# Full-row score products with zero rows, and SSM inputs from an ordered copy

## The chip, the cores and the metric

One NeuronCore of a Trainium2 chip runs the whole program in one launch. The metric is the device time of one execution in microseconds (us); less is better. Engines are named as in the profile: PE is TensorE (PEld its weight loads), DVE is VectorE, ACT is ScalarE, POOL is GpSimd and SP the queue that issues most transfers.

## What is computed

The reference is a stack of three transformer layers on 512 tokens of width 1024 (528 with 16 meta tokens in the first two layers). Each layer is a feed-forward block, a mixer and a second feed-forward block. Only the mixers matter here:

- Mixer A (first layer): differential attention, 8 heads with two score maps each, `logits = q·k * scale + bias` over 64 numbers a head, softmax, `p0 - lam*p1`, times V. All queries see the 16 meta keys besides the real ones.
- Mixer B (second layer): sparse latent attention with 16 heads, which shares the helper for the 16 meta keys.
- Mixer C (third layer): windowed attention with 12 heads in 3 patterns, scores over 64 numbers a head again, beside a state-space branch (SSM) whose input is `u = x @ w[:, :512]`, cross-attention and gates.

```python
bu_re = jnp.einsum('blgh,gph->blgp', uf, bbar_re)     # u in 32 groups of 16
logits = jnp.einsum("bqhmd,bkhmd->bmhqk", qb, k).astype(jnp.float32) * scale + bias
pd = p[:, 0] - lam_full * p[:, 1]
```

## The kernel before

Every fp32 operand is split into a high and a low part (ACT casts the high part, DVE subtracts for the low one), and a product is three matmuls: high·high, high·low, low·high. The helper `mm3` (L108, L110, L112) does this for projections; where "a projection" is counted below, it is 24 matmuls of 512 columns. `loadw` fetches a weight through `st` (L85), casts it (L88, ACT) and subtracts (L90, DVE); its pool `wp` holds four weight pairs.

Scores have only 64 rows to contract, so the kernel packs. `stack_q` puts the high part of a head's q in 64 rows and the low part in the other 64 of one tile; `stack_k` puts the high part of k in both halves, and the low part in a third tile, in the head's own 64 rows. `scores` then is two matmuls: L475 over all 128 rows (both parts of q with the high part of k) and L476 over 64 rows alone (the high part of q with the low part of k). The two add up in one PSUM bank:

```python
s.nc.tensor.matmul(p, Q[b][:, cq], K[b][:, ck], start=True, stop=False)       # L475
s.nc.tensor.matmul(p, Q[b][r, cq], K[2][r, ck], start=False, stop=True)       # L476, r = 64 rows
```

`pv` multiplies probabilities and values. Its first two matmuls are those of the 16 meta keys: L836 over 48 rows (high and low part of the probabilities, `PM`, at rows 0 and 32) and L837 over 16 rows. The rest (L841) has 128 rows. Mixer B has its own matmul over the 48-row tiles (L1098). `pm_tile` (L817) makes these tiles and clears them once.

In mixer C two heads go with each index j. A slot (j, b) is the attention of head b of j: for four blocks of 128 queries and three patterns a score pair into one of three banks, a DVE instruction that adds the bias strip and keeps the running maximum (L1511), one exponential per block on ACT (L1517), a reciprocal and a scaling on DVE (L1519, L1520); then transposes on PE (L1546), the split of what they give (L455 on ACT, L456 on DVE), and the products with V (L1552), at the end `fold`. A slot pair, slots (j, 0) and (j, 1), has 24 score pairs, 54 transposes and 68 products with V.

The program text of mixer C is: projections of j = 0, V of j = 0 (`vproj`, L1485), slots (0, 0) and (0, 1), `ssm_u` for the first half of the SSM inputs, projections and V of j = 1, slots (1, 0) and (1, 1), `ssm_u` for the second half, then the SSM itself (L1711, L1724 and on) with gate projections between its parts. `ssm_u` has positions in four classes modulo 4, since the SSM wants four neighbouring positions side by side. It takes every fourth column of `xh` and `xl` as the stationary operand, so that a weight load reads with a stride of four elements, and multiplies with 256 columns of the weight: 96 matmuls for each half (L1690).

A scheduler orders each engine's instructions from this text; an engine then works through its own list in order. So matmuls that wait for nothing (projections, `ssm_u`) are put between those of a slot that wait for DVE and ACT. It can do this only if their weight is loaded, which needs one of the four buffers of `wp`.

Of the kernel before, what the change touches and what calls it, by code (L numbers as in the profile page):

```python
# [8 lines left out]
F32 = mybir.dt.float32  # L9
# [25 lines left out]
class Kern:  # L35
# [430 lines left out]
    def stack_k(s, K, p, c):  # L466

        for b, (r, o) in enumerate(HALVES):
            s.split(K[b][r, c], K[2][r, c], p[r])
            s.nc.scalar.copy(K[b][o, c], p[r])  # L470

    def scores(s, p, Q, K, b, cq, ck):

        r = HALVES[b][0]
        s.nc.tensor.matmul(p, Q[b][:, cq], K[b][:, ck], start=True, stop=False)  # L475
        s.nc.tensor.matmul(p, Q[b][r, cq], K[2][r, ck], start=False, stop=True)  # L476

# [101 lines left out]
    def mixer_a(s, x, gnext):  # L579
# [6 lines left out]
        with ExitStack() as es:  # L586
# [29 lines left out]
            om = o1.tile([128, 128], F32, name="om")  # L616
            sm = o1.tile([16, 2, 8], F32, name="sm")
# [13 lines left out]
            def fin(hd, i, ac):  # L631
                if i < 2:
                    sd[hd, i] = [o2.tile([128, 528], F32R, tag="%s%d" % ("qk"[i], a), name="%ss" % "qk"[i])
                                 for a in range(2 + i)]
                if i == 0:
# [30 lines left out]
                else:  # L666
# [8 lines left out]
                    v.tensor_copy(VM[:, hd], raw[:, 0:16])  # L675
                    mh, ml = vms[hd % 3], o2.tile([16, 128], F32R, tag="vml", name="vml", bufs=3)
                    s.split(mh[0:16], ml, pt[:16, :128])
                    nc.scalar.copy(mh[32:48], pt[:16, :128])
# [46 lines left out]
            def meta():  # L725

                MB = o1.tile([16, 16, 16], F32, name="mb")
                for q in range(16):
# [3 lines left out]
                                                        ap=[[w - 1, 16], [1, 16]]))  # L732
                P = o1.tile([16, 16, 16], F32, name="pmeta")
                bc = (lambda q: q.unsqueeze(2).to_broadcast((16, q.shape[1], 16)))
# [31 lines left out]
                for hd in range(8):  # L766
                    nc.tensor.matmul(p[:, hd * 16:hd * 16 + 16], vt[hd // 4][:, hd % 4 * 128:hd % 4 * 128 + 128], PmT[:, hd * 16:hd * 16 + 16], start=True,
                                     stop=True)
                nc.scalar.copy(om, p[:, :128])
                sq = s.t528("sq", "sqm")[:, :128]  # L770
# [3 lines left out]
                r = s.rsqrt([(p, 0, 128)], 128, sq, lnexp=True)  # L774
                v.scalar_tensor_tensor(om, om, pr[:, 2:3], r, op0=ALU.mult, op1=ALU.mult)

            s.run(T, proj(0), 3)
            s.banks(**ATTN)
            s.run(T, proj(1)[2:], 0)
            for hd in range(8):  # L780
                attn(hd)
                if hd < 7:
                    s.run(T, proj(hd + 1)[:2 if hd < 6 else 3], 0)
                if hd < 5:
                    s.run(T, proj(hd + 2)[2:], 0)
                if hd == 6:
                    meta()
# [43 lines left out]
    def pv(s, po, PT, PM, vh, vl, mh, ml, vsl, msl, M, hv):  # L831
# [596 lines left out]
    def mixer_c(s, x, gnext):  # L1428
# [15 lines left out]
        with ExitStack() as es0:  # L1444
            c0 = es0.enter_context(tc.tile_pool(name="c0", bufs=1))
            DO = [c0.tile([128, 2, 512], F32R, name="do%d" % i) for i in range(2)]
            cu = es0.enter_context(tc.tile_pool(name="cu", bufs=2))
            todo = []
# [4 lines left out]
            with ExitStack() as es:  # L1453
# [3 lines left out]
                s.stat = es.enter_context(tc.tile_pool(name="dst", bufs=12))  # L1457
                qk, V = {}, {}

                def job(kind, gr, j):  # L1460
# [7 lines left out]
                    def fin(acs):  # L1468
                        t = [d1.tile([128, 512], F32R, tag="%s%d%d" % (kind, gr, q), name="%ss" % kind)
                             for q in range(2 if kind == "q" else 3)]  # L1470
# [202 lines left out]

    def ssm_u(s, pool, xh, xl, hf):

        nc = s.nc
        v = nc.vector
        ws = [s.loadw(s.I["w_u"][hf, a], 1024) for a in range(2)]
        U4 = pool.tile([128, 1024], F32, tag="u4", name="u4")
        U4 = U4.rearrange("p (g r h) -> p g r h", r=4, h=16)  # L1680
        for rp in range(2):
            pu = s.bank()
            for r in (2 * rp, 2 * rp + 1):
                for k in range(8):
                    wh, wl = ws[k // 4]
                    sl = slice((k % 4) * 256, (k % 4) * 256 + 256)
# [5 lines left out]
            for r in (2 * rp, 2 * rp + 1):  # L1692
                q = pu[:, r % 2 * 256:r % 2 * 256 + 256].rearrange("p (g h) -> p g h", g=16)
                if r % 2:
                    v.tensor_copy(U4[:, :, 3 - r], q)
                else:
                    nc.scalar.copy(U4[:, :, 3 - r], q)
        return U4
# [139 lines left out]
def prepare(v):  # L1838
    def t(a):
        return np.ascontiguousarray(a)  # L1840
# [48 lines left out]
    w = v["w_in_2"][0]  # L1889
    A["w_u"] = t(w[:, :512].reshape(2, 4, 128, 2, 256).transpose(3, 0, 2, 1, 4).reshape(2, 2, 128, 1024))  # L1890
    A["w_q"] = pack(w[:, 512:1280])
# [56 lines left out]
```

## Time and profile before

| | |
|---|---|
| runs | 3524.14, 3529.34, 3533.30 us; median 3529.34 |
| the profiled execution | 3530.96 us, its span 3529.2 us |
| PE busy, share of the span | 3385.9 us, 96% |
| DVE, ACT, POOL | 75%, 46%, 9% |
| mean granted clock of PE | 0.975 of full speed |

Times in rows are counted from the start of the span. A matmul's own duration overlaps with the next one's; the pace of PE is the distance from one start to the next. What stands as idle before an instruction is told with what released it.

### The profile page before, as it was taken

How to read it: one execution, taken by the hardware profiler on the slowest of the kernel's cores; microseconds unless marked ns; L12 is line 12 of the kernel's file. 1: busy time of each engine (PE TensorE's matmuls, PEld its weight loads, DVE VectorE, ACT ScalarE, POOL GpSimd, SP SyncE). 2: the span in 40 equal slices, each digit the busy share in tenths (PEclk: the TensorE clock that was granted, in tenths of full speed). 3: DMA queues.
4: the chain of work that ended last, by engine and by line, in shares of the span. 5: the costliest groups of instructions: out<-in, count | busy, mean ns of one | idle time of the engine just before them, and what ended most of it. 6: DMA issues, size and time to landing. Idle time of an engine off the chain costs nothing.

```text
span 3529.2 us, 60108 instructions
## 1 busy us (share of the span) xinstructions
PE 3385.9 (96%) x23568; PEld 3121.1 (88%) x23568; DVE 2647.1 (75%) x5495; ACT 1640.7 (46%) x3026; POOL 311.2 (9%) x494
## 2 busy tenths in 40 slices
PE   7999999999999999988999799999999999999998
PEld 7999888899999999977878699999998878889997
DVE  8777766699978987688978588787774555388776
ACT  5444566544445444555654344444453433344443
POOL 0100122100000000054520001000000000010000
PEclk9999999999999999988999899999998999999999
DMA  3532322123323432231212334233232233242331
GB/s 132 165 100 84 96 64 67 47 83 111 116 91 106 138 110 91 73 116 41 61 66 81 110 113 129 92 109 103 92 97 74 71 120 101 80 130 92 106 102 60
DMA packets 133645, 336.95 MB, mean 95 GB/s; under 512 B 27042, under 2 KB 39106, under 8 KB 133360
## 3 DMA queue, kind: packets, MB, share of 16 engines
q1 hardware_dynamic: 114336, 311.38, 28.3%
q0 software_dynamic: 19024, 21.72, 2.1%
q8 instruction: 185, 3.03, 0.4%
q14 instruction: 100, 0.82, 0.1%
HBM read 320.00 MB, written 24.35 MB: 98 GB/s over the span
## 4 chain that ended last, share of the span: by engine, by line
PE 86%; DVE 7%; DMA 3%; ACT 2%; issue 2%; POOL 0%; SPq 0%; DVEq 0%; ACTq 0%; POOLq 0%
PE bank L401 33%; PE bank L108 14%; PE bank L110 14%; PE bank L112 14%; PE bank L1690 1%; PE bank L476 1%; PE bank L1088 1%; PE bank L1485 1%; PE bank L475 1%; PE bank L1101 1%; DVE wl L90 1%; PE bank L841 1%; DMA xr<-in_oh 1%; PE bank L1008 1%; DMA xr<-dP 0%
## 5 line engine op out<-in xcount | busy, mean ns | idle before, releaser
L401 PE MATMUL bank<-xh,wl 128*128 128x264 f32 (+1 forms) x1920 | 539.8, 284 | 13.1 <-DVE wl L359 13.1
L88 ACT CAST wh<-st 128x1024 fp32r<-128x1024 f32 (+5 forms) x385 | 319.2, 840 | 497.2 <-PE bank L110 266.7
L401 PE MATMUL bank<-xh,wh 128*128 128x264 f32 (+1 forms) x1920 | 543.3, 284 | 4.5 <-ACT wh L358 4.5
L90 DVE TENSOR_TENSOR wl<-st,wh 128x1024 fp32r<-128x1024 f32 (+4 forms) x373 | 363.9, 982 | 151.1 <-ACT wh L88 150.2
L110 PE MATMUL bank<-gl,wh 128*128 128x264 f32 (+2 forms) x1638 | 447.1, 316 | 0.0
L112 PE MATMUL bank<-gh,wl 128*128 128x264 f32 (+2 forms) x1638 | 444.0, 316 | 0.0
L108 PE MATMUL bank<-gh,wh 128*128 128x264 f32 (+2 forms) x1638 | 442.4, 318 | 0.4 <-DVE h L261 0.3
L108 PE MATMUL bank<-xh,wh 128*128 128x264 f32 (+3 forms) x1344 | 416.6, 325 | 10.6 <-ACT xh L455 3.2
L110 PE MATMUL bank<-xl,wh 128*128 128x264 f32 (+3 forms) x1344 | 425.1, 322 | 0.1
L112 PE MATMUL bank<-xh,wl 128*128 128x264 f32 (+3 forms) x1344 | 420.0, 319 | 0.0
L401 PE MATMUL bank<-xl,wh 128*128 128x264 f32 (+1 forms) x1440 | 408.1, 284 | 0.0
L401 PEld LDWEIGHTS bank<-xh,wl 128*128 128x128 f32 x1920 | 362.1, 190 | 14.4 <-DVE wl L359 13.5
L401 PEld LDWEIGHTS bank<-xh,wh 128*128 128x128 f32 x1920 | 363.7, 190 | 6.2 <-ACT wh L358 5.6
L401 PE MATMUL bank<-xq,wah 128*128 128x264 f32 (+1 forms) x1920 | 361.6, 284 | 0.5 <-ACT cc L406 0.3
L401 PEld LDWEIGHTS bank<-xq,wah 128*128 128x128 f32 x1920 | 299.8, 190 | 2.9 <-ACT sl L410 0.6
L110 PEld LDWEIGHTS bank<-gl,wh 128*128 128x128 f32 x1638 | 280.7, 189 | 21.8 <-issue 1.3
L108 PEld LDWEIGHTS bank<-gh,wh 128*128 128x128 f32 x1638 | 278.8, 189 | 22.3 <-ACT wah L358 1.1
L112 PEld LDWEIGHTS bank<-gh,wl 128*128 128x128 f32 x1638 | 279.0, 188 | 21.5 <-issue 1.6
L108 PEld LDWEIGHTS bank<-xh,wh 128*128 128x128 f32 (+1 forms) x1344 | 250.7, 192 | 35.2 <-ACT xh L455 3.6
L401 PEld LDWEIGHTS bank<-xl,wh 128*128 128x128 f32 x1440 | 272.7, 189 | 0.8 <-issue 0.5
L110 PEld LDWEIGHTS bank<-xl,wh 128*128 128x128 f32 (+1 forms) x1344 | 255.7, 191 | 20.1 <-issue 2.1
L401 PE MATMUL bank<-xq,wal 128*128 128x264 f32 (+1 forms) x960 | 271.6, 283 | 0.0
(591 smaller groups left out, 7681.7 us busy)
## 6 DMA issues: line engine op xcount, KB each, us to landing
st<-in_wi SPq DMA_DIRECT2D x144, 512.0 KB, 4.1
fu<-in_wi SPq DMA_DIRECT2D x120, 512.0 KB, 3.5
st<-in_wo SPq DMA_DIRECT2D x96, 384.0 KB, 3.1
st<-in_wo SPq DMA_DIRECT2D x96, 320.0 KB, 3.0
st<-in_a_w_in SPq DMA_DIRECT2D x24, 512.0 KB, 3.5
st<-in_w_out SPq DMA_DIRECT2D x24, 512.0 KB, 3.5
st<-in_w_g SPq DMA_DIRECT2D x24, 512.0 KB, 3.5
strip<-kA SPq DMA_DIRECT2D x32, 264.0 KB, 2.8
```

The source lines that it names most:

```text
L88: nc.scalar.copy(wh[:rows, :n], st[:rows, :n])
L90: s.wl.tensor_tensor(wl[:rows, :n], st[:rows, :n], wh[:rows, :n].bitcast(F32), op=ALU.subtract)
L108: nc.tensor.matmul(p[:m], a, xh(k, t0, n), start=st, stop=False)
L110: nc.tensor.matmul(p[:m], a, xl(k, t0, n), start=False, stop=False)
L112: nc.tensor.matmul(p[:m], b, xh(k, t0, n), start=False, stop=en)
L401: nc.tensor.matmul(B, a[:, w], q[c][:, k], start=first and k == 0 and z == 0, stop=k == 3 and z == 2, skip_group_check=not first)
L475: s.nc.tensor.matmul(p, Q[b][:, cq], K[b][:, ck], start=True, stop=False)
L476: s.nc.tensor.matmul(p, Q[b][r, cq], K[2][r, ck], start=False, stop=True)
L841: nc.tensor.matmul(po[:M, c], a[:, vsl(j)], q[:, k], start=False, stop=j == 0 and n == 2)
L1008: nc.tensor.matmul(pv[:n, z * 256:z * 256 + 256], c[:, k, t0:t0 + n], wv[:, k * 256:k * 256 + 256], start=q == 0, stop=q == 5)
L1088: nc.tensor.matmul(ps[0][:, :n], q[:, k * 512 + i * 128:k * 512 + i * 128 + 128], c[:, k, k0:k0 + n], start=z == 0, stop=z == 5)
L1101: nc.tensor.matmul(po[:, hv], vs[:, j, m], PT[i // 2][q][:, j * 256:j * 256 + 256], start=False, stop=j == 0 and q == 1)
```

## The change

The low part of k is kept in two tiles, one for each head of a pair, 128 rows high: 64 rows hold it, the other 64 are set to zero once (`low_keys`, by POOL) and never written again. The second score matmul takes all 128 rows. The tiles of the meta keys and their probabilities become 128 rows high with zeros below, so both meta matmuls take 128 rows, in mixer B too. Some small tiles of `meta` in mixer A now borrow room from tiles that exist. In mixer C `ssm_u` is called once, for both halves, after the last slot and after the pools of the attention are closed: for each of the eight k it copies `xh` (ACT) and `xl` (DVE) into tiles in which the four classes are contiguous, and multiplies with 512 columns.

```diff
@@ stack_k, scores
-            s.split(K[b][r, c], K[2][r, c], p[r])
+            s.split(K[b][r, c], K[2 + b][r, c], p[r])
...
-        s.nc.tensor.matmul(p, Q[b][r, cq], K[2][r, ck], start=False, stop=True)
+        s.nc.tensor.matmul(p, Q[b][:, cq], K[2 + b][:, ck], start=False, stop=True)
+    def low_keys(s, pool, n, name):
+        ts = [pool.tile([128, n], F32R, name="%s%d" % (name, b)) for b in range(2)]
+        for t, (_, o) in zip(ts, HALVES):
+            s.nc.gpsimd.memset(t[o].bitcast(F32), 0.0)
+        return ts
@@ mixer_a
-            vms = [s.pm_tile(o1, 128, "vm%d" % i) for i in range(3)]
+            vms = [[s.pm_tile(o1, 128, "vm%d%d" % (i, a)) for a in range(2)] for i in range(3)]
+            KL = [s.low_keys(o1, 528, "kl%d" % i) for i in range(2)]
@@ pm_tile, pv
-        t = pool.tile([48, n], F32R, name=name)
+        t = pool.tile([128, n], F32R, name=name)
...
-        nc.tensor.matmul(po[:M, c], ml[:, msl], PM[0:16, c], start=False, stop=False)
+        nc.tensor.matmul(po[:M, c], ml[:, msl], PM[:, c], start=False, stop=False)
@@ mixer_c
+                KL = [s.low_keys(d1, 512, "kl%d" % gr) for gr in range(3)]
...
-                U4 = [s.ssm_u(cu, xh, xl, 0)]
...
                 slot(1, 1)
-                U4.append(s.ssm_u(cu, xh, xl, 1))
+                s.banks(m=[0, 1, 2, 3])
+            cu = es0.enter_context(tc.tile_pool(name="cu", bufs=2))
+            with tc.tile_pool(name="xp", bufs=2) as xp:
+                U4 = s.ssm_u(cu, xp, xh, xl)
@@ ssm_u
-                    ah = xh[:, k].rearrange("p (m r) -> p r m", r=4)[:, r]
-                    al = xl[:, k].rearrange("p (m r) -> p r m", r=4)[:, r]
-                    for z, (a, b) in enumerate(((ah, wh), (ah, wl), (al, wh))):
-                        nc.tensor.matmul(pu[:, r % 2 * 256:r % 2 * 256 + 256], a, b[:, sl], start=k == 0 and z == 0,
-                                         stop=k == 7 and z == 2)
+        pu = [s.bank() for _ in range(4)]
+        for kc in range(4):
+            wh, wl = s.loadw(s.I["w_u"][kc], 1024)
+            for a in range(2):
+                k = 2 * kc + a
+                X = [xp.tile([128, 4, 128], F32R, tag="xp%d" % i, name="xp%d" % i) for i in range(2)]
+                nc.scalar.copy(X[0], xh[:, k].rearrange("p (m r) -> p r m", r=4).bitcast(F32))
+                v.tensor_copy(X[1], xl[:, k].rearrange("p (m r) -> p r m", r=4).bitcast(F32))
+                c = slice(a * 512, a * 512 + 512)
+                for r in range(4):
+                    for z, (x, w) in enumerate(((0, wh), (0, wl), (1, wh))):
+                        nc.tensor.matmul(pu[r], X[x][:, r], w[:, c], start=k == 0 and z == 0, stop=k == 7 and z == 2)
```

In the three mixers' score and meta matmuls the scheduler leaves the order as it was, but for a few rows near mixer A's end. In mixer C it does not. The first place is PE's list from the first scores of slot (1, 0) on; `wh`, `wl`, `xh` and `xl` belong to `ssm_u`, `ks` and `kl` are keys, `qs` queries. Before:

```order
L475 MATMUL bank4_77<-ks_30206,qs_30170 128x256
L476 MATMUL bank4_77<-ks_30208,qs_30170 128x256
L475 MATMUL bank2_75<-ks_30056,qs_30020 128x256
L476 MATMUL bank2_75<-ks_30058,qs_30020 128x256
L475 MATMUL bank3_76<-ks_30131,qs_30095 128x256
L476 MATMUL bank3_76<-ks_30133,qs_30095 128x256
L1690 MATMUL bank0_73<-wh_30694,xh_28669 128x256
L1690 MATMUL bank0_73<-wl_30696,xh_28669 128x256
L1690 MATMUL bank0_73<-wh_30694,xl_28670 128x256
```

The same place in the changed kernel, where L474 and L475 are the two score matmuls:

```order
L474 MATMUL bank4_77<-ks_30094,qs_30058 128x256
L475 MATMUL bank4_77<-kl20_29061,qs_30058 128x256
L474 MATMUL bank2_75<-ks_29946,qs_29910 128x256
L475 MATMUL bank2_75<-kl00_29053,qs_29910 128x256
L474 MATMUL bank3_76<-ks_30020,qs_29984 128x256
L475 MATMUL bank3_76<-kl10_29057,qs_29984 128x256
L474 MATMUL bank2_75<-ks_29946,qs_29910 128x256
L475 MATMUL bank2_75<-kl00_29053,qs_29910 128x256
L474 MATMUL bank3_76<-ks_30020,qs_29984 128x256
L475 MATMUL bank3_76<-kl10_29057,qs_29984 128x256
```

Where 96 matmuls of `ssm_u` and 48 of two gate projections stood between the scores and products of slots (1, 0) and (1, 1), there is now nothing of either kind: PE's list has the slots alone, then 96 matmuls of `ssm_u`, then a projection (21 rows), 8 transposes of the SSM, a projection and 8 transposes. In slots (0, 0) and (0, 1) the 144 matmuls of the j = 1 projections stay: 48 among the first seven score pairs, then none for some three fifths of the slot pair's instructions, then 96.

The second place is ACT's list at the end of slot (1, 1) in the changed kernel; `dth` is the high part of transposed probabilities, `xp0` the ordered copy of `xh`, `do0` the attention's output, `wh` a gate's weight:

```order
L455 CAST dth_30551<-bank5_78 128x512
L455 CAST dth_30551<-bank6_79 128x384
L861 COPY fold_30574<-bank7_80 64x512
L1696 CAST xp0_30597<-xh_28666 128x512
L1696 CAST xp0_30613<-xh_28666 128x512
L455 CAST do0_29039<-fold_30574 64x512
L1696 CAST xp0_30635<-xh_28666 128x512
L1696 CAST xp0_30651<-xh_28666 128x512
L88 CAST wh_30945<-st_30943 128x1024
```

The first copy stands behind the `fold` of the last slot, which reads the bank that the last products with V fill. The weights of `ssm_u` were cast earlier, three among the projections of j = 1 and one after V; all four pairs stay in `wp` until `ssm_u` has used them, and the gates' weights come behind.

## Rows read from the trace of the kernel before

**Rows 1.** The page: the chain of work that ended last, by engine.

```profile
PE 86%; DVE 7%; DMA 3%; ACT 2%; issue 2%; POOL 0%; SPq 0%; DVEq 0%; ACTq 0%; POOLq 0%
```

**Rows 2.** Timeline of PE in mixer A: start us, duration, line, out<-in, shape.

```profile
426.02 0.34 PE L475 MATMUL bank<-ks,qs 128*128 128x400 f32 x1
426.29 0.44 PE L476 MATMUL bank<-ks,qs 64*128 64x400 f32 x1
426.67 0.39 PE L108 MATMUL bank<-xh,wh 128*128 128x264 f32 x1
426.89 0.29 PE L110 MATMUL bank<-xl,wh 128*128 128x264 f32 x1
```

**Rows 3.** Timeline of PE in mixer C, where a 128-row matmul parts a pair.

```profile
2719.54 0.28 PE L475 MATMUL bank<-ks,qs 128*128 128x256 f32 x1
2719.65 0.28 PE L1552 MATMUL bank<-dth,vs 128*128 128x256 f32 x1
2719.87 0.38 PE L476 MATMUL bank<-ks,qs 64*128 64x256 f32 x1
```

**Rows 4.** Timeline of PE in mixer A at the meta matmuls.

```profile
517.26 0.38 PE L836 MATMUL bank<-pm,vm 48*128 48x256 f32 x1
517.57 0.38 PE L837 MATMUL bank<-pm,vml 16*128 16x256 f32 x1
517.88 0.50 PE L841 MATMUL bank<-pt,vh 128*128 128x256 f32 x2
```

**Rows 5.** Views of three lines: count, ns min/median/max, first and last start, forms.

```profile
L476 PE MATMUL bank<-ks,qs x128: 378/385/792, 419.8 to 2837.0; 64*128 64x256 f32 x48, 64*128 64x264 f32 x32, 64*128 64x400 f32 x16, 64*128 64x272 f32 x16
L837 PE MATMUL bank<-pm,vml x16: 377/380/576, 442.4 to 685.1; 16*128 16x256 f32 x16
L1098 PE MATMUL bank<-pm,vm x32: 378/381/384, 1612.7 to 1831.9; 48*128 48x256 f32 x32
```

**Rows 6.** Windows in mixers A, B: length, PE, PEld, DVE, ACT, POOL busy; clock.

```profile
440.00:640.00 200.00, 198.10 (x1303) 168.93 (x1302) 137.42 (x376) 133.33 (x325) 47.15 (x84) 0.98 0.19 61
1610.00:1835.00 225.00, 204.25 (x1297) 177.57 (x1295) 186.99 (x537) 133.97 (x351) 105.50 (x149) 0.97 0.16 45
```

**Rows 7.** Loads of L1690 and L475 (views of lines); timeline of L1690, of a projection.

```profile
L1690 PEld LDWEIGHTS bank<-wh,xh x64: 307/333/337, 2670.3 to 2811.7; 128*128 128x128 f32 x64
L475 PEld LDWEIGHTS bank<-ks,qs x128: 186/188/330, 419.4 to 2836.7; 128*128 128x128 f32 x128
2672.27 0.40 PE L1690 MATMUL bank<-wh,xl 128*128 128x256 f32 x1
2672.51 0.40 PE L1690 MATMUL bank<-wh,xh 128*128 128x256 f32 x1
...
2648.63 0.39 PE L108 MATMUL bank<-xh,wh 128*128 128x512 f32 x1
2648.86 0.40 PE L110 MATMUL bank<-xl,wh 128*128 128x512 f32 x1
```

**Rows 8.** Windows of mixer C, columns as in rows 6.

```profile
2669.50:2706.60 37.10, 37.10 (x134) 31.09 (x132) 13.50 (x41) 9.29 (x15) 0.00 (x0) 0.74 0.22 70
2726.30:2733.30 7.00, 7.00 (x41) 5.16 (x39) 5.04 (x12) 3.17 (x8) 0.64 (x5) 1.00 0.21 57
2762.30:2779.60 17.30, 17.30 (x102) 17.30 (x101) 8.69 (x12) 7.97 (x13) 0.34 (x2) 1.00 0.32 99
2779.60:2853.50 73.90, 68.51 (x325) 56.58 (x323) 36.60 (x103) 25.78 (x47) 5.40 (x24) 0.95 0.16 51
2840.20:2853.50 13.30, 9.06 (x55) 7.45 (x53) 6.97 (x15) 5.78 (x13) 2.71 (x9) 0.87 0.03 11
```

**Rows 9.** DVE's weight splits inside 2779.6 to 2853.5: count, busy us, mean ns.

```profile
L90 DVE TENSOR_TENSOR wl<-st,wh 128x1024 fp32r<-128x1024 f32 x5 | 6.1, 1223 | 3.5 <-ACT wh L88 3.5
```

**Rows 10.** ACT's copy after slot (1, 1), and POOL's first work in mixer A.

```profile
L853 ACT COPY fold<-bank 64x512 f32<-64x512 f32 x1 | 0.6, 577 | 1.8 <-PE bank L1552 1.8
...
412.25 0.70 POOL L703 TENSOR_SCALAR pa<-strip,R 128x528 f32<-128x528 f32 x1 [23.04 <-DVE lt L1794]
```

More of the change, by code (lines that the diff above doesn't have):

```diff
@@ L468, in stack_k @@
         for b, (r, o) in enumerate(HALVES):
-            s.split(K[b][r, c], K[2][r, c], p[r])
+            s.split(K[b][r, c], K[2 + b][r, c], p[r])
             s.nc.scalar.copy(K[b][o, c], p[r])
     def scores(s, p, Q, K, b, cq, ck):
-        r = HALVES[b][0]
         s.nc.tensor.matmul(p, Q[b][:, cq], K[b][:, ck], start=True, stop=False)
-        s.nc.tensor.matmul(p, Q[b][r, cq], K[2][r, ck], start=False, stop=True)
+        s.nc.tensor.matmul(p, Q[b][:, cq], K[2 + b][:, ck], start=False, stop=True)
[4 more added lines that the diff above has]
+        return ts
     def split_pool(s, h_ap, l_ap, src, t):
@@ L612, in mixer_a @@
             PM = s.pm_tile(o1, 512)
-            vms = [s.pm_tile(o1, 128, "vm%d" % i) for i in range(3)]
+            vms = [[s.pm_tile(o1, 128, "vm%d%d" % (i, a)) for a in range(2)] for i in range(3)]
+            KL = [s.low_keys(o1, 528, "kl%d" % i) for i in range(2)]
             QM, KM = o1.tile([128, 8, 16], F32, name="qm"), o1.tile([128, 8, 16], F32, name="km")
             VM = o1.tile([128, 8, 16], F32, name="vmeta")
-            om = o1.tile([128, 128], F32, name="om")
             sm = o1.tile([16, 2, 8], F32, name="sm")
@@ L633, in fin @@
                     sd[hd, i] = [o2.tile([128, 528], F32R, tag="%s%d" % ("qk"[i], a), name="%ss" % "qk"[i])
-                                 for a in range(2 + i)]
+                                 for a in range(2)] + (KL[hd % 2] if i else [])
                 if i == 0:
@@ L675, in fin @@
                     v.tensor_copy(VM[:, hd], raw[:, 0:16])
-                    mh, ml = vms[hd % 3], o2.tile([16, 128], F32R, tag="vml", name="vml", bufs=3)
-                    s.split(mh[0:16], ml, pt[:16, :128])
+                    mh, ml = vms[hd % 3]
+                    s.split(mh[0:16], ml[0:16], pt[:16, :128])
                     nc.scalar.copy(mh[32:48], pt[:16, :128])
@@ L725, in meta @@
             def meta():
-                MB = o1.tile([16, 16, 16], F32, name="mb")
+                mt = s.tmp.tile([128, 528], F32, tag="acc", name="mt", bufs=1)[:16, :512]
+                MB, P = [mt[:, a * 256:a * 256 + 256].rearrange("p (a b) -> p a b", a=16) for a in range(2)]
                 for q in range(16):
@@ L732, in meta @@
                                                         ap=[[w - 1, 16], [1, 16]]))
-                P = o1.tile([16, 16, 16], F32, name="pmeta")
                 bc = (lambda q: q.unsqueeze(2).to_broadcast((16, q.shape[1], 16)))
@@ L768, in meta @@
                                      stop=True)
+                om = s.t528("ra", "om")[:, :128]
                 nc.scalar.copy(om, p[:, :128])
@@ L775, in meta @@
                 v.scalar_tensor_tensor(om, om, pr[:, 2:3], r, op0=ALU.mult, op1=ALU.mult)
+                return om
             s.run(T, proj(0), 3)
@@ L786, in mixer_a @@
                 if hd == 6:
-                    meta()
+                    om = meta()
                     y = s.newx(T)
@@ L1446, in mixer_c @@
             DO = [c0.tile([128, 2, 512], F32R, name="do%d" % i) for i in range(2)]
-            cu = es0.enter_context(tc.tile_pool(name="cu", bufs=2))
             todo = []
@@ L1469, in fin @@
                         t = [d1.tile([128, 512], F32R, tag="%s%d%d" % (kind, gr, q), name="%ss" % kind)
-                             for q in range(2 if kind == "q" else 3)]
+                             for q in range(2)] + (KL[gr] if kind == "k" else [])
                         for (p, t0, n) in acs[0]:
@@ L1672, in xattn, with ssm_u @@
         s.split(XA[0][:, hd], XA[1][:, hd], po)
-    def ssm_u(s, pool, xh, xl, hf):
+    def ssm_u(s, pool, xp, xh, xl):
         nc = s.nc
         v = nc.vector
[L1678 to L1686, printed above, removed]
-                    ah = xh[:, k].rearrange("p (m r) -> p r m", r=4)[:, r]
-                    al = xl[:, k].rearrange("p (m r) -> p r m", r=4)[:, r]
-                    for z, (a, b) in enumerate(((ah, wh), (ah, wl), (al, wh))):
-                        nc.tensor.matmul(pu[:, r % 2 * 256:r % 2 * 256 + 256], a, b[:, sl], start=k == 0 and z == 0,
-                                         stop=k == 7 and z == 2)
-            for r in (2 * rp, 2 * rp + 1):
-                q = pu[:, r % 2 * 256:r % 2 * 256 + 256].rearrange("p (g h) -> p g h", g=16)
+        U4 = [pool.tile([128, 1024], F32, tag="u4", name="u4") for _ in range(2)]
+        U4 = [q.rearrange("p (g r h) -> p g r h", r=4, h=16) for q in U4]
+        pu = [s.bank() for _ in range(4)]
[10 more added lines that the diff above has]
+                        nc.tensor.matmul(pu[r], X[x][:, r], w[:, c], start=k == 0 and z == 0, stop=k == 7 and z == 2)
+        for hf in range(2):
+            for r in range(4):
+                q = pu[r][:, hf * 256:hf * 256 + 256].rearrange("p (g h) -> p g h", g=16)
@@ L1694, in ssm_u @@
                 if r % 2:
-                    v.tensor_copy(U4[:, :, 3 - r], q)
+                    v.tensor_copy(U4[hf][:, :, 3 - r], q)
                 else:
-                    nc.scalar.copy(U4[:, :, 3 - r], q)
+                    nc.scalar.copy(U4[hf][:, :, 3 - r], q)
         return U4
@@ L1889, in prepare @@
     w = v["w_in_2"][0]
-    A["w_u"] = t(w[:, :512].reshape(2, 4, 128, 2, 256).transpose(3, 0, 2, 1, 4).reshape(2, 2, 128, 1024))
+    A["w_u"] = t(w[:, :512].reshape(4, 2, 128, 512).transpose(0, 2, 1, 3).reshape(4, 128, 1024))
     A["w_q"] = pack(w[:, 512:1280])
```

## The prediction

> **What bounds the kernel now.** I read the chain of waits first: 86% of what ended last is TensorE [rows 1]. Then the timeline of PE, for the pace, since a matmul's own duration says little. Ordinary matmuls of 256 columns start 0.11 to 0.12 us apart (L475 to L1552 in [rows 3]), those of 512 columns 0.23 us [rows 7]. A score pair in mixer A breaks this: from L475 to L476 0.27, from there to the next matmul 0.38, and to the one after 0.22, together 0.87 us [rows 2]. At the ordinary pace, 0.18 for 400 columns (0.12 x 400/264), it would be 0.18 + 0.18 + 0.12 = 0.48. So a pair costs 0.39 us more than its columns. [Rows 3] show where that comes from: there a 128-row matmul stands between L475 and L476, and after L475 no time is lost (0.11), but 0.22 pass before the 64-row L476. The loss is in going from 128 rows to 64 and back. The meta matmuls, over 48 and 16 rows, lose alike: 0.31 each in place of 0.12 [rows 4]. Equal duration of 64-row and 128-row forms is not what I rely on; what counts is that the step between forms goes.
>
> Next, who else is near the limit. In mixer A DVE has 137 of 200 us, ACT 133, PE 198; in mixer B DVE has 187 of 225 against PE's 204 [rows 6]. So A is PE's, B is nearly DVE's.
>
> Last, mixer C by stretches [rows 8]. PE looks full, but part of it is filler: `ssm_u` and projections put into gaps of the slots. The row to look at is 2726.3 to 2733.3, where PE had slot work alone: DVE was busy 5.04 of 7.0 us, 0.72. In the last 13.3 us of slot (1, 1), again without filler and with nothing of a next slot, it was 0.52. [...]
>
> **The change, part by part.** The sum is made against the profiled execution, 3530.96 us, which is 1.6 us above the median of the three runs; I leave that difference out.
>
> *Score pairs and meta matmuls of A.* There are 128 pairs [rows 5], 48 of them in C (24 in each of two slot pairs), so 80 in A: 80 x 0.39 = 31.2 us. The 16 meta couples (L836 and L837): 0.62 in place of 0.24 [rows 4], and 0.1 for the step back as in [rows 2]: 0.48 x 16 = 7.7. Together 39 us on PE. Number and columns of the matmuls stay. What can stay behind is DVE's: at 39 us less of about 270, its share rises from 0.69 to 0.80, below full, and the order of the list stays. I take 33, with 39 and 20 as ends (20: half, if PE then waits where it now loses time anyway).
>
> *Meta matmuls of B.* 32 [rows 5], one step in and one out, 0.19 + 0.1 as above: 9.6 us on PE. With DVE at 0.83 [rows 6] I take half, 5; ends 0 and 9.6.
>
> *Clears by POOL.* Ten tiles of keys and larger meta tiles, some 3 us more before mixer A's heads and 3 before C's. POOL stands idle 23 us before its first work in A [rows 10], so nothing. Larger tiles take room, not time.
>
> *`ssm_u`.* Before: 192 matmuls of 256 columns at 0.24 us [rows 7], 46 us. Their loads, with a stride of four, take 333 ns where packed ones take 188 [rows 7]. After: 96 of 512 columns with packed loads, at the pace of a projection, 0.23: 22.3 us. [...]
>
> The copies: 8 on ACT, 8 on DVE, of 128x512. The trace has none with this stride out of SBUF; a copy of half the partitions and 512 columns takes 0.58 [rows 10], DVE's subtraction of 1024 columns 1.22 [rows 9], so 0.6 to 1.2. A k has 12 matmuls, 2.8 us, so at either end they lie beside PE's work, except the first: ACT's list has it behind `fold` (0.58), which waits for the last product with V. I take 0.6 + 0.7 and 0.2 for hand-overs: 1.5 us bare. The four weights of `ssm_u` are cast beside V of j = 1, where ACT has 8.0 and DVE 8.7 of 17.3 us [rows 8]; two more pairs fit. Their transfers are four of the same size before and after, issued by SP earlier against the gates' and later against the strips of slot (0, 1); DMA is 0.32 busy there [rows 8], so nothing.
>
> *Mixer C as a whole*, from the first score (2669.5) to the last product with V (2853.5): 184.0 us. What moves is the filler. `ssm_u` leaves the slots, and because its four weights hold all of `wp`, the two gate projections (48 matmuls) leave slots (1, 0) and (1, 1) too. So the slots must run at their own speed there. A slot pair's own DVE time: 36.6 us in [rows 8], less 6.1 of weight splits [rows 9] and some 2.5 of V, `ssm_u` and SSM copies, is 28. Its own PE time without the steps is about 22 (48 score matmuls at some 0.15, 122 others at 0.12). So without filler DVE sets the speed, at the occupancy of 0.72 that the one bare row shows.
>
> - Slots (0, 0), (0, 1): first 48 projection matmuls with seven pairs, 11.1 + 1.9 = 13.0; then three fifths of the pair without filler, 0.6 x 28 / 0.72 = 23.3; then 96 projection matmuls with the rest, 22.3 + 8.7 = 31.0. Sum 67.3.
> - V of j = 1, as before: 17.3 [rows 8].
> - Slots (1, 0), (1, 1), no filler: 28 less the tail's 7.0 is 21, / 0.72 = 29.2, and the tail of 13.3 as before: 42.5.
> - `ssm_u`: 1.5 + 22.3 = 23.8. The 48 gate matmuls, later: 11.1.
>
> The sum is 162.0, 22 less. For the clock I take off 4: bare slots do less on PE than the ones that already ran at 0.74. Gain 18 us. Ends: occupancy 1 makes the two bare stretches 6.5 and 8.2 shorter, and without the 4 the gain is 36.7; the tail's 0.52 makes them 8.8 and 10.9 longer, and it is a loss of 2. The 48 pairs of C lose some 18 us in steps too; that doesn't come on top, since I counted PE's time here without them and DVE sets most of it.
>
> Sum: 33 + 5 + 18 = 56, so **3475 us**.
>
> **The rivals.**
>
> *C gives its part back.* The slots without filler run as the tail does, DVE at 0.52. For it: in the tail PE, DVE and ACT wait in turn. Against it: two slots overlap, and the bare row with overlap has 0.72. C is then 2 us slower, A and B keep 38: 3495.
>
> *All of it comes out.* DVE fills up, nothing waits: 39 + 9.6 + 36.7 = 85, 3446. For it: in A PE is busy nearly all the time. Against it: DVE was nowhere above 0.83 in these rows.
>
> *The steps do not go.* The time lost is tied to something else in L476 (the second operand, the bank), and zero rows don't help. [Rows 3] speak against it, and that L836, L837 and L1098 lose alike with other operands. A and B then give nothing, and C between -2 and 18 less what its filled parts lose, some 5: 3526.
>
> [...]
>
> **How the numbers follow.** A measurement of this kernel can tell about 0.3%, 10.6 us, from no change. Chances: the forecast 0.63; C gives back 0.20; all comes out 0.08; the steps stay 0.05; slower by the clock 0.04. The first three are faster by more than that, the fourth is within it. So 0.91, 0.05, 0.04. The range: down to 3448, by most of the second rival; up to 3507, which is C giving back (3495) with 12 us less from A, near its lower end. That leaves out the last two and the extremes.
>
> **What would show it.** The second score matmul as 128 rows, 0.12 us after the first where nothing waits, in A, B's meta matmuls likewise; the stretch of A's heads some 33 us shorter with DVE near 0.8. `ssm_u` as 96 matmuls 0.23 us apart with loads of 188 ns. PE with clear gaps in slots (1, 0) and (1, 1), DVE about 0.7 busy, the two slots in about 42 us. If A's stretch shrinks by under 20 us, the price of a step or its place on the path was wrong; if the two bare slots take over 55 us, or the clock stands at 0.5 through `ssm_u`, the mixer C part was.

## The result, and the profile after

The changed kernel takes 3469.6 us (median; 3463.97 to 3470.35), the kernel before 3526.7 us beside it: 0.9833, with an interval of [0.9813, 0.9853]. In a second comparison (e14 below) it was 0.9821 [0.9806, 0.9836]. The forecast was 3475 us.

The page of the changed kernel, its first lines (span, then busy time of the engines):

```profile
span 3467.7 us, 59965 instructions
PE 3308.4 (95%) x23472; PEld 3084.5 (89%) x23472; DVE 2646.4 (76%) x5503; ACT 1650.5 (48%) x3034; POOL 319.0 (9%) x507
```

PE is busy 77.5 us less than before (3385.9 us), DVE as long as it was (2647.1 us). The timeline of PE at a pair of 400 columns in mixer A, which answers to [rows 2], and at a meta couple ([rows 4]):

```profile
427.26 0.34 PE L474 MATMUL bank<-ks,qs 128*128 128x400 f32 x1
427.44 0.34 PE L475 MATMUL bank<-kl,qs 128*128 128x400 f32 x1
427.62 0.28 PE L108 MATMUL bank<-xh,wh 128*128 128x264 f32 x1
427.74 0.28 PE L110 MATMUL bank<-xl,wh 128*128 128x264 f32 x1
...
440.95 0.39 PE L844 MATMUL bank<-pm,vm 128*128 128x256 f32 x1
441.17 0.28 PE L845 MATMUL bank<-pm,vm 128*128 128x256 f32 x1
441.29 0.40 PE L849 MATMUL bank<-pt,vh 128*128 128x256 f32 x2
```

From L474 to the second matmul behind the pair it is 0.48 us, where it was 0.87: the step is gone, to the hundredth. The meta couple takes 0.34 in place of 0.62.

To see where the 61.5 us between the two spans arise, equal DVE instructions of both traces can be compared by their starts. Before A's heads the changed kernel is 1.8 us late; behind them it is 25.3 early; through mixer B it gets from 23.8 to 28.1; through mixer C to 61.4, and stays there. So A gave 27 us, B 4, C 33, between these two executions. The execution of the kernel before that was profiled is 4.2 us above the median of its four runs, and e1 below shows that C's 33 us are some 5 too many for that reason.

Windows of the changed kernel: A and B inside (columns and places of [rows 6]), then mixer C: slots (0, \*), the bare part of these, V of j = 1, slots (1, \*), the tail of slot (1, 1), `ssm_u`:

```profile
441.50:616.00 174.50, 169.87 (x1296) 159.25 (x1294) 134.71 (x376) 132.31 (x323) 47.29 (x83) 1.00 0.23 72
1586.00:1802.00 216.00, 194.54 (x1288) 174.54 (x1287) 185.96 (x529) 132.00 (x348) 105.59 (x149) 0.98 0.16 45
2641.70:2704.00 62.30, 58.56 (x312) 48.80 (x311) 42.28 (x108) 33.25 (x57) 4.44 (x26) 0.97 0.27 83
2654.20:2675.40 21.20, 17.46 (x102) 14.20 (x101) 17.71 (x56) 12.30 (x25) 2.16 (x13) 0.92 0.19 57
2704.00:2721.30 17.30, 17.30 (x102) 17.30 (x101) 8.70 (x12) 7.96 (x13) 0.34 (x2) 1.00 0.32 96
2721.30:2758.60 37.30, 30.29 (x171) 25.01 (x170) 29.07 (x93) 19.15 (x36) 4.89 (x24) 0.86 0.13 41
2745.00:2758.60 13.60, 10.38 (x52) 8.63 (x51) 7.52 (x18) 6.13 (x11) 2.04 (x10) 0.75 0.00 1
2758.60:2782.90 24.30, 22.45 (x99) 18.00 (x97) 10.44 (x16) 13.59 (x16) 0.00 (x0) 1.00 0.51 163
```

A's inside has DVE at 134.71 of 174.5, 0.77, with the same 376 DVE instructions as in [rows 6]. In B DVE has 186 of 216, 0.86. In C the two slot pairs take 62.3 and 37.3 us, and PE now has idle time in them, as the order said. DVE has 17.71 of 21.20 in the bare part, 0.84, and in slots (1, \*) without the tail 21.55 of 23.7, 0.91.

The same stretch of A before and after, from the first score on; it leaves out the last scores and the products with V of the last two heads:

```profile
419.40:649.50 230.10, 226.30 (x1490) 192.63 (x1488) 160.30 (x446) 152.30 (x374) 54.24 (x96) 0.99 0.19 62
```

```profile
421.50:624.50 203.00, 195.62 (x1490) 182.92 (x1488) 158.20 (x445) 152.13 (x374) 55.46 (x96) 1.00 0.22 70
```

1490 matmuls either way, and 27.1 us less. To the end of the last product with V it is 29.3 us less, of which some 2 are lost again right behind it:

```profile
419.40:686.40 267.00, 260.01 (x1697) 219.21 (x1695) 183.42 (x515) 171.22 (x424) 58.12 (x102) 0.96 0.17 54
```

```profile
421.50:659.20 237.70, 227.29 (x1726) 211.01 (x1724) 181.57 (x514) 171.03 (x424) 59.35 (x102) 0.98 0.19 61
```

Last `ssm_u`: the view of its line (loads; 96 matmuls in all), and the timeline, where the first matmul waits for the ordered copy:

```profile
L1701 PEld LDWEIGHTS bank<-wh,xp x64: 187/188/189, 2760.5 to 2782.2; 128*128 128x128 f32 x64
...
2760.55 0.50 PE L1701 MATMUL bank<-wh,xp 128*128 128x512 f32 x1 [1.80 <-ACT xp L1696]
2760.89 0.40 PE L1701 MATMUL bank<-wl,xp 128*128 128x512 f32 x1
2761.12 0.63 PE L1701 MATMUL bank<-wh,xp 128*128 128x512 f32 x2
```

### The profile page after: what moved, and what is told of

Its sections match the earlier page's. It is cut to its first block, busy times and chain, and to the rows that moved or that the text cites. A ratio compares the mean times of both kernels' runs of the same rounds, so it can differ in the third digit from the quotient of the medians.

```text
span 3467.7 us, 59965 instructions
## 1 busy us (share of the span) xinstructions
PE 3308.4 (95%) x23472; PEld 3084.5 (89%) x23472; DVE 2646.4 (76%) x5503; ACT 1650.5 (48%) x3034; POOL 319.0 (9%) x507
## 5 line engine op out<-in xcount | busy, mean ns | idle before, releaser
L108 PE MATMUL bank<-gh,wh 128*128 128x264 f32 (+2 forms) x1638 | 442.5, 318 | 0.3 <-DVE sq L414 0.2
L108 PE MATMUL bank<-xh,wh 128*128 128x264 f32 (+3 forms) x1344 | 413.0, 322 | 13.2 <-DVE sqo L141 3.4
L108 PEld LDWEIGHTS bank<-gh,wh 128*128 128x128 f32 x1638 | 278.7, 188 | 22.2 <-ACT wah L358 1.1
L108 PEld LDWEIGHTS bank<-xh,wh 128*128 128x128 f32 (+1 forms) x1344 | 249.2, 191 | 36.5 <-DVE qs L456 4.0
```

Of the source, the lines that this page charges most:

```text
L108: nc.tensor.matmul(p[:m], a, xh(k, t0, n), start=st, stop=False)
```

## The experiments

The theory that went into the first four runs was the prediction's: A and B give what they give by the steps, and C by its filler's new place and form, with its own steps hidden behind DVE. The rival: every step lies on the path, in C too.

**e1_ab_only.** A and B as changed, mixer C's scores and `ssm_u` as before. The main lines, against the changed kernel:

```diff
-                KL = [s.low_keys(d1, 512, "kl%d" % gr) for gr in range(3)]
...
+                U4 = [s.ssm_u(cu, xh, xl, 0)]
...
-                U4 = s.ssm_u(cu, xp, xh, xl)
+                U4.append(s.ssm_u(cu, xh, xl, 1))
```

> The full-row score and meta matmuls in mixers A and B alone; mixer C as in the kernel before (64-row second score matmul, two calls of ssm_u between the slots). If the steps between row forms are what A and B gained by: A ends 27 us sooner, B another 4 to 5, mixer C takes the 184 us from first score to last product with V that it took before, and the time is 3527 - 32 = 3495. Rival, that A's and B's shift is only time moved and is handed back later: mixer C starts no sooner than before, 3527.

Measured: 3497.1 us, 0.9913 [0.9898, 0.9928]; 31 us of the gain are A's and B's. The changed kernel differs from e1 in mixer C alone, and is 27.5 us faster: that is C's part by medians, where the two profiles above gave 33. What lies between the two shows in slots (0, \*), which have the same program in the kernel before and in e1 (first before, then e1):

```profile
2669.50:2762.30 92.80, 92.80 (x410) 75.84 (x409) 46.51 (x113) 36.24 (x61) 4.38 (x26) 0.87 0.22 68
```

```profile
2639.80:2725.90 86.10, 86.10 (x408) 71.69 (x407) 46.30 (x112) 36.32 (x62) 4.40 (x26) 1.00 0.24 72
```

The granted clock was 0.87 in the one and 1.00 in the other, with 6.7 us between them, and the forecast was made against the slower one. So C did not take its 184 us again, as was expected of e1. Over all of C e1 is 5 us shorter than the kernel before, by the starts of its DVE instructions.

**e4_a64.** The changed kernel with A's second score matmul over its 64 rows again, from the same tiles (`half` is set in A's call alone):

```diff
+        r = HALVES[b][0] if half else slice(0, 128)
...
-        s.nc.tensor.matmul(p, Q[b][:, cq], K[2 + b][:, ck], start=False, stop=True)
+        s.nc.tensor.matmul(p, Q[b][r, cq], K[2 + b][r, ck], start=False, stop=True)
```

> The changed kernel with the second score matmul of mixer A over 64 rows again, from the same new tiles; its meta matmuls keep 128 rows. If the number of rows is the cause: from L474 to its partner 0.2 to 0.3 us again, and A gives back what the score pairs earned, 20 to 24 us, 3492. Rival, that the gain came with the tiles (own tile for each head, no shared low part): no change, 3470.

Measured: 3495.6 us (3490.78 to 3497.76), 26 us over the changed kernel. PE's timeline there:

```profile
427.54 0.34 PE L475 MATMUL bank<-ks,qs 128*128 128x400 f32 x1
427.81 0.44 PE L476 MATMUL bank<-kl,qs 64*128 64x400 f32 x1
428.18 0.39 PE L108 MATMUL bank<-xh,wh 128*128 128x264 f32 x1
428.41 0.29 PE L110 MATMUL bank<-xl,wh 128*128 128x264 f32 x1
```

Again 0.87 us a pair, with the new tiles and every other matmul as changed. So it is the 64 rows that cost, not the tile, the bank or the operand, and A's part is theirs alone but for a microsecond or so: 26 of 80 x 0.39 = 31. A lower clock may have a part in these 26 us, which no run separates from the steps: in this stretch of e4's heads it was 0.97, where the changed kernel has 1.00 from 441.5 to 616.0:

```profile
441.50:642.00 200.50, 197.47 (x1332) 172.53 (x1332) 141.18 (x388) 134.96 (x331) 47.13 (x88) 0.97 0.21 63
```

The timeline shows where the time goes: 0.27 us from L475 to the 64 rows of L476 and 0.37 from these to the next matmul, where the changed kernel, with 128 rows throughout, has 0.18 and 0.18.

**e2_ssm_only.** The new `ssm_u` alone, all steps as before. Two lines, against the changed kernel:

```diff
-            s.split(K[b][r, c], K[2 + b][r, c], p[r])
+            s.split(K[b][r, c], K[2][r, c], p[r])
...
-        s.nc.tensor.matmul(p, Q[b][:, cq], K[2 + b][:, ck], start=False, stop=True)
+        s.nc.tensor.matmul(p, Q[b][r, cq], K[2][r, ck], start=False, stop=True)
```

> The new ssm_u (ordered copy, 512 columns, after the last slot) alone; all score and meta matmuls as before, with 64, 48 and 16 rows. If DVE sets the speed of slots without filler, lost steps of PE there are hidden and count only where filler is left: A and B as before, mixer C 25 to 29 us shorter of the 33 that the changed kernel shows there, 3500. Rival, that every step in mixer C is on the path (48 pairs x 0.38 = 18 us): 33 - 18 = 15 us, 3512. Second rival, that ssm_u gains nothing by itself: 3527.

Measured: 3515.8 us, 0.9966 [0.9954, 0.9977]: 12 us, not the 28 that my theory had for it, and near the 15 of the rival by which every step in C is on the path. Its slots (0, \*) and (1, \*), at lower granted clocks than in the changed kernel, take 18.8 us more than the 62.3 and 37.3 there:

```profile
2673.50:2746.60 73.10, 72.40 (x312) 55.05 (x311) 42.84 (x108) 33.62 (x58) 5.20 (x26) 0.86 0.24 71
2763.90:2809.20 45.30, 41.12 (x171) 29.18 (x170) 30.05 (x93) 19.47 (x36) 4.54 (x24) 0.77 0.11 33
```

**e3_c64** and **e9_c64_again.** The changed kernel with C's second score matmul over 64 rows, the edit of e4 in `slot`. One program, measured twice.

> The changed kernel with the second score matmul of mixer C over 64 rows again (the same tiles, the zero rows not read); A, B and ssm_u stay changed. If DVE sets the speed of the bare slots: 4 to 8 us more, 3474 to 3478, with the loss in the parts of slots (0, 0) and (0, 1) that have projections between. Rival, every step on the path: 18 us more, 3488.

> The same program as e3_c64 (the changed kernel with mixer C's second score matmul over 64 rows again), run once more because its four runs lay between 3478 and 3494 us. The part of the loss that is steps must be there in every run: 48 x 0.39 = 18.7 us if each is on the path, giving 3488; the part that is the granted clock may differ from run to run. Theory 1 (the steps themselves, all on the path, cost the 20 us): the median comes out at 3486 to 3492 again and low runs like 3478 are rare. Theory 2 (steps cost 5 to 10 us, and the rest is a lower clock in the slots that comes in some executions): the runs spread again between 3477 and 3494, and in the profile the time lost against the changed kernel grows with the length of the low-clock stretches.

Measured: 3489.4 us (3477.91 to 3494.28), then 3485.2 (3483.86 to 3488.39): 20 and 16 us over the changed kernel. e9's median is just below theory 1 and within theory 2, without the spread that this one asked for. My theory of the first four runs falls: C's steps are worth about as much as all else in C. Slots (0, \*) and (1, \*) in e3, then in e9:

```profile
2644.90:2717.00 72.10, 70.81 (x312) 54.10 (x311) 42.69 (x108) 33.49 (x58) 4.57 (x26) 0.88 0.23 72
2734.30:2781.10 46.80, 42.62 (x170) 29.84 (x170) 29.64 (x93) 19.60 (x36) 4.55 (x24) 0.74 0.10 32
```

```profile
2640.50:2709.10 68.60, 66.97 (x311) 51.07 (x311) 42.49 (x108) 33.42 (x57) 4.42 (x26) 0.95 0.26 75
2726.50:2772.80 46.30, 42.38 (x171) 29.74 (x169) 29.61 (x93) 19.60 (x36) 4.55 (x24) 0.74 0.11 33
```

DVE's work is that of the changed kernel (42.3 and 29.1). What differs besides the steps is the granted clock: 0.88 and 0.95 in the same code of slots (0, \*), with 3.5 us between them, and 0.74 in slots (1, \*) where the changed kernel has 0.86. Windows of half a microsecond of the changed kernel, from 2600 to 2900 us, have 1.00 in 569 of 600 and 0.50 in 25. With these two levels in all three executions the clocks make, as an estimate, some 14 us at the lower level in the slots of the changed kernel, 31 in e9 and 42 in e3, and the slots are 15.3 and 19.3 us longer: that much of theory 2 holds. Steps and clock act together here; e13 below parts them for slots (1, \*).

**e5_no_copy.** The changed kernel without the ordered copy:

```diff
-                X = [xp.tile([128, 4, 128], F32R, tag="xp%d" % i, name="xp%d" % i) for i in range(2)]
-                nc.scalar.copy(X[0], xh[:, k].rearrange("p (m r) -> p r m", r=4).bitcast(F32))
-                v.tensor_copy(X[1], xl[:, k].rearrange("p (m r) -> p r m", r=4).bitcast(F32))
+                X = [q[:, k].rearrange("p (m r) -> p r m", r=4) for q in (xh, xl)]
```

> The changed kernel without the ordered copy: the 96 matmuls of 512 columns of ssm_u take their stationary operand straight from the stored layout (every fourth element), as the kernel before does. My theory: a 512-column matmul takes 0.232 us on the path and hides a strided load, whose own pace was 0.24 us in the kernel before; so the 512 columns alone (half as many matmuls) bring the gain of ssm_u, the copy brings nothing, and the time is that of the changed kernel or 1 to 2 us less (the first matmul no longer waits for a copy): 3466 to 3471 us, 96 matmuls in 22.3 to 23.1 us. Rival: the copy is what brings it, and a strided load of 0.333 us shows wherever it is longer than the matmul it stands beside: 96 x (0.333 - 0.232) = 9.7 us more, 3479 us.

Measured: 3464.8 us (3462.37 to 3466.08), 0.9816 [0.9802, 0.983]. It is no slower, so the copy brings nothing here. But the edit did more than was expected. By the program text the copy's tiles come behind the pools of the attention, whose memory the slots hold until they end; without it the scheduler puts all 96 matmuls among the scores of slots (1, \*), from 2724 to 2770 us. So the run is no clean measure of the copy alone. Of the loads: they take 309 ns again, and matmuls that follow one another start 0.237 us apart (median of 83 distances), against 0.229 with packed loads. A matmul of 512 columns hides all but 8 ns of a strided load; one of 256 columns, at 0.24 [rows 7] against 0.12, did not.

**e11_split_u.** That placement made on purpose. `ssm_p` holds the loop over k for two of the four classes, with the strided operand; only the copies out of PSUM stay behind the slots:

```diff
                 slot(1, 1)
+                uw = [s.loadw(s.I["w_u"][kc], 1024) for kc in range(4)]
+                pu = s.ssm_p(uw, xh, xl, 0)
-                s.banks(m=[0, 1, 2, 3])
+                s.banks(m=[2, 3])
             cu = es0.enter_context(tc.tile_pool(name="cu", bufs=2))
-            with tc.tile_pool(name="xp", bufs=2) as xp:
-                U4 = s.ssm_u(cu, xp, xh, xl)
+            U4 = s.ssm_u(cu, uw, pu, xh, xl)
...
```

> The changed kernel with the 96 SSM matmuls of 512 columns (strided stationary operand, no copy) written ahead of the end of slots (1,*), two residues on banks 0 and 1 and two on banks 2 and 3, which those slots leave free; only the copies out of PSUM wait for the memory of the slots. The order on TensorE then puts them between the steps of slots (1,*). My theory: in the changed kernel these slots take 37.3 us in which TensorE works 30.3 us at a granted clock of 0.86, and ssm_u stands behind them with 24.3 us; as fillers the matmuls use the idle time and hold the clock, so the two stages together take 50 to 53 us in place of 61.6: 3458 to 3462 us. Rival 1 (DVE is the bound of these slots, and the four weight splits of 1 us each now lie in them too): gain of 4 to 6 us, 3464. Rival 2 (the matmuls get in the way of the steps; slots (1,*) grow by all 22 us): 3469 to 3471.

Measured: 3462.2 us, 0.981 [0.9795, 0.9824]. Slots (1, \*), with `ssm_u` in them:

```profile
2719.60:2771.60 52.00, 48.87 (x266) 44.52 (x265) 35.03 (x97) 22.96 (x40) 4.17 (x24) 1.00 0.22 69
```

52.0 us in place of 37.3 + 24.3 = 61.6, as expected, and the granted clock stands at 1.00 where the bare slots had 0.86. Of these 9.6 us, 6 to 7 reach the end (5.9 in the next comparison, 7.4 in this one). e5 had come near it by accident: 52.1 us for the same stretch.

**e14_after_again** and **e15_split_again.** The changed kernel and e11's program side by side.

> The changed kernel itself, beside e15_split_again on the same chip: it gave 3464 to 3470 us in its four runs. Expected again 3466 to 3472. In mixer C the slots (1,*) and ssm_u behind them should take 61 to 62 us together.

> The program of e11_split_u once more (ssm_u as filler in slots (1,*)), for a comparison with the changed kernel in the same call. If the gain of 7 us is real: 3459 to 3466 us, the two medians 5 to 9 us apart, slots (1,*) with ssm_u in them 52 us at a granted clock of 1.00. If it was the difference of two calls: medians within 3 us of each other.

Measured: 3467.3 us (3466.32 to 3472.66) and 3461.4 (3460.62 to 3464.15); 0.9821 [0.9806, 0.9836] and 0.9802 [0.9788, 0.9816] of the kernel before. The five runs of one lie below the four of the other, 5.9 us between the medians. This version is the fastest of all, by a little.

**e13_u_c64.** e11 with C's second score matmul over 64 rows, the edit of e3:

> e11_split_u (ssm_u as filler in slots (1,*)) with mixer C's second score matmul over 64 rows again. With the slots bare, those 48 matmuls cost 15.6 and 20 us in two runs, of which the granted clock had a part: the slots (0,*) grew by 6.3 and 9.8 us, the slots (1,*) by 9.1 and 9.6, with low-clock stretches of 6.8 to 17.1 us. Theory: where TensorE is full the step itself is on the path at the 0.39 us of mixer A (24 x 0.39 = 9.4 us in slots (1,*)) and the clock stays up there; slots (0,*), still bare, give 6 to 10 again: 15 to 19 us in all, 3477 to 3481, with no long low-clock stretch in slots (1,*). Rival: most of the loss in slots (1,*) was the clock, which the fillers now hold, and the steps hide behind DVE: 6 to 10 us in all, 3468 to 3472.

Measured: 3477.4 us (3475.77 to 3480.23), 15 over e11. Slots (0, \*) and (1, \*):

```profile
2641.30:2713.30 72.00, 70.70 (x312) 53.84 (x311) 42.72 (x108) 33.42 (x57) 4.55 (x26) 0.88 0.23 73
2730.60:2788.60 58.00, 56.38 (x268) 45.99 (x266) 35.32 (x97) 22.95 (x40) 4.05 (x24) 1.00 0.20 62
```

The sum is as my theory had it, its parts are not. Slots (1, \*) ran at 1.00 with the steps and without, and grew by 6.0 us (58.0 against 52.0): 24 steps at 0.25 us, the one price of a step in C at an equal clock, from one profiled execution each; 0.39 even where PE has filler was too much. Slots (0, \*), where the clock went to 0.88, grew by 10.0 (from 62.0 in e11), of which 6 are steps by that price and 4 would be the clock. In e9's slots (0, \*), at 0.95, the price comes out again: 6.3 us for 24 steps. With 12 us for all 48, e9's 15.3 us have 3 left for the clock and e3's 19.3 have 7. This split is an estimate, since a step costs more at the lower level. Here is PE at a granted 0.50, in the changed kernel and in e3:

```profile
2662.91 0.41 PE L475 MATMUL bank<-kl,qs 128*128 128x256 f32 x1
2663.13 0.41 PE L474 MATMUL bank<-ks,qs 128*128 128x256 f32 x1
2663.34 0.41 PE L475 MATMUL bank<-kl,qs 128*128 128x256 f32 x1
```

```profile
2668.72 0.58 PE L476 MATMUL bank<-kl,qs 64*128 64x256 f32 x1
2669.23 0.58 PE L475 MATMUL bank<-ks,qs 128*128 128x256 f32 x1
2669.74 0.58 PE L476 MATMUL bank<-kl,qs 64*128 64x256 f32 x1
```

A pair takes 0.43 us without the step and 1.02 with it, so a step is 0.59 of PE's timeline there, against 0.39 in [rows 2].

**e8_a3banks** and **e12_a_s3t1.** Could A lose its last waits? Two other ways to give out its PSUM banks:

```diff
-            s.banks(**ATTN)
+            s.banks(m=[0, 1], s=[2, 3, 4], t=[5, 6], o=[7])
```

in e8, and in e12

```diff
-            s.banks(**ATTN)
+            s.banks(m=[0, 1, 2], s=[3, 4, 5], t=[6], o=[7])
```

`ATTN` gives three to the fillers (m), two to scores (s), two to transposes (t), one to the product with V (o).

> The changed kernel with mixer A's eight PSUM banks given out as in mixer C: two for the fillers, three for scores, two for transposes, one for the product with V. Without the steps, the score matmuls of A still lose some 10 us to waits, most of them for a score bank that DVE has not read yet. My theory: a third score bank takes out about half of these, 4 to 6 us, and the time is 3464 to 3466 us. Rival 1: DVE is simply behind (0.77 busy in that stage), a bank more only moves the wait, and the time stays at 3469 to 3470. Rival 2: the filler projections lose their banks and the stage gets longer by a few us: 3473 or more.

> The changed kernel with mixer A's banks given out as three for the fillers (as they are), three for scores in place of two, and one for transposes in place of two. e8_a3banks showed that the fillers can't spare a bank; this takes it from the transposes instead. Theory: the 10 us that A's score matmuls still wait are waits for a score bank that DVE has not read, and a third one takes out 3 to 6 us: 3464 to 3467. Rival: the single transpose bank makes every group of transposes wait for the split of the group before (DVE and ACT), some 8 heads x 7 groups x 0.3 to 0.5 us = 17 to 28 us: 3486 to 3498.

Measured: 3528.4 us and 3501.0 us. Either bank taken away costs far more than a third one for scores could give: 59 us and 31 over the changed kernel. A stretch of e8 with about the work of the changed kernel's 441.5 to 616.0 (columns of [rows 6]), the waits of PE in it, and those of PEld in e12 from 418 to 720 (us in total, times, longest):

```profile
441.50:676.00 234.50, 196.45 (x1321) 176.78 (x1320) 137.98 (x385) 133.19 (x329) 44.81 (x87) 0.92 0.18 53
```

```profile
PE bank L108 <- DVE sqa L141: 19.5, 6, 3.3
PE bank L844 <- DVE pm L456: 5.1, 6, 0.9
PE bank L474 <- DVE st L580: 4.7, 8, 0.8
PE bank L835 <- DVE pt L456: 4.1, 5, 0.8
```

```profile
PEld bank L821 <- DVE sqo L141: 7.2, 3, 4.4
PEld bank L844 <- DVE pm L456: 6.9, 7, 1.4
PEld bank L821 <- DVE pt L456: 4.9, 5, 1.8
```

In e8 the fillers (L108) wait for a bank of their own, and then, as I read these waits, nothing covers the scores, which still wait (L474); in e12 it is the transposes (L821). PE is idle for 38.1 us in the stretch of e8, against 4.6 in the changed kernel's, and the granted clock is 0.92 against 1.00; what each of the two makes of the 59 us was not separated. e12 keeps pace with the changed kernel up to 600 us (1334 matmuls against 1343 from 420 on) and loses its time behind: from 600 to 720 PE is busy for 94.7 us against 110.2, at 0.83 against 0.94. In the changed kernel the waits of PEld at L474 for DVE are 3.1 us up to 625, and 7.0 with the last heads, so there was less to win than the 10 us that I had put down to them.

## Why the prediction was right, and where it was not

- **The price of a step and its place in A: right.** 0.39 us by [rows 2]; the pair after takes the 0.48 that was worked out, and e4 brings both the step and 26 us back. The 33 us were 27. Of the two terms the pairs gave 26 of their 31.2, and the meta matmuls next to nothing of the 7.7 counted for them: their couple takes 0.34 on PE's timeline where it took 0.62, but in e4, where they alone are changed in A, A is only 0.3 us shorter by its DVE starts. DVE's share ended at 0.77 (0.76 over all heads), where 0.80 was said.
- **B, 5 us: 4**, by the shift of its instructions; not tested by a run of its own. The same measure gives between 0.2 and 6.0 in the other runs with the changed B, and -1.7 in e2, where B is as before, so the 4 is uncertain by some 2 us. e1's 31 us are A and B together and agree. The 9.6 us of the upper end are 32 x 0.29 = 9.3.
- **`ssm_u`: right in size, wrong in reason.** 24.3 us against 23.8 foretold, its loads at 188 ns. That the copy earns this fell with e5: it is the 512 columns that hide the strided load (0.237 us from start to start with it, 0.229 with a packed one). What the copy does is to hold `ssm_u` back behind the slots, and that costs the 6 to 7 us that e11 and e15 get back; that its memory is the reason is read from the program text.
- **Mixer C: the step that was mis-sized.** Foretold were 162.0 us for the pieces and 4 more for the clock, a gain of 18; the pieces took 62.3 + 17.3 + 37.3 + 24.3 + 11.1 = 152.3 (the last, the gate matmuls, at the forecast's price), a gain of 32 on the profiled execution and of some 27 on C as e1 has it. Three terms account for it. First the occupancy of DVE in bare slots: 0.72 was taken from the row 2726.3 to 2733.3 [rows 8], and it came out at 0.84 and 0.91. That row itself held five pairs with their steps; at e13's 0.25 us they make 1.25 of its 7.0 us, and 5.04 of the other 5.75 is 0.88. So the sentence that the steps' loss "doesn't come on top, since I counted PE's time here without them and DVE sets most of it" was wrong in its premise: the occupancy was read where the steps were, and left them in. Runs e3, e9 and e13 show what they are worth, 15 to 20 us with what the clock adds. The bare part of slots (0, \*) was 2.1 us shorter than foretold for it, slots (1, \*) 5.2. Second the parts of slots (0, \*) with projections, foretold with 13.0 and 31.0 us: together 2.9 less. Third the 4 us taken off for the clock, a term that no run shows: the bare slots did fall, to 0.92 and 0.86, but `ssm_u` behind them ran at 1.00, and the slots came out shorter than foretold all the same.
- **Two errors of opposite sign** stand in the sum, then: A 6 too high, C some 10 too low (27.5 by e1, against 18). With B's 1 and the 2 us that the changed kernel was late before mixer A they nearly cancel: 56 us were forecast, and by medians it is 57.1. Of the 5 us by which 3475 missed, 4 come from the base, the profiled execution at 3530.96 in place of the median of 3526.7. That the sum came so close is luck: its terms lay further off.
- **The rivals.** That the steps would not go is refuted by the timeline and e4. That C gives its part back did not come, nor a kernel slower by the clock, which was 1.00 through `ssm_u`. The kernel came between the forecast and "all of it comes out"; the 0.91 of DVE in slots (1, \*) is near that rival's full DVE, while A's 0.77 is not.

## What to carry to other kernels

Where TensorE is as full as in mixer A here (198 of 200 us [rows 6]), pad a short contraction with zero rows that are set once, so that all matmuls of a stretch have one row form (a pair took 0.48 us in place of 0.87); look for the loss in the distance between starts, on both sides of the odd form, not in its duration. An occupancy that is to stand for a stretch after a change must be read from a row without the thing that the change removes, or with its price taken out. Before a copy is added to make an operand contiguous, see whether a longer matmul hides the strided load (512 columns hid all but 8 ns of it in e5), and ask what the copy's memory keeps from moving up.

## What the runs showed that was not expected

- A step costs 0.25 us in C's slots with filler (24 of them, e13), 0.33 in A (26 us for 80, with what the clock has in them), though it takes 0.39 on PE's timeline. Part of it falls into time in which PE would have waited: PE was idle for 3.1 us of e11's 52.0, and for 1.6 of e13's 58.0. That is 1.5 of the 3.4 us by which 24 x 0.39 exceeds 6.0; the rest is open.
- In bare slots the steps go with a lower granted clock: 0.86 to 0.95 in slots (0, \*) (e2, e3, e9, e13) against 0.97, and 0.74 to 0.77 in slots (1, \*) against 0.86, and not alike from run to run: e3's four lie between 3477.9 and 3494.3 us. With filler between the scores of slots (1, \*) it held 1.00, with the steps or without (e11, e13); in slots (0, \*) with steps and the filler of before it was 0.87 in one execution and 1.00 in another (before, e1). Why stretches with steps, in which PE counts as busier (70.81 of 72.10 us in slots (0, \*) of e3, 58.56 of 62.30 in the changed kernel), get the lower clock was not settled.
- One PSUM bank taken from the filler projections of mixer A and given to the scores costs 59 us, as much as the whole change brings.
